# A hybrid retention/NATTEN encoder layer on one core: the output weights of mixing split once, and element-wise work moved from GpSimd to VectorE

## The chip, the cores and the metric

The kernel runs on one core of a Trainium2 chip. The metric is device time in microseconds of one execution, the median of several. The core's engines run side by side, each with its own queue of instructions in a fixed order: TensorE (PE; PEld loads its weights), VectorE (DVE), ScalarE (ACT), GpSimd (POOL), and SyncE (SP), which issues most DMAs. They wait for each other with semaphores. TensorE reads its operands from SBUF and writes PSUM banks of 128 x 512 fp32.

## The reference: what is computed

One layer of an encoder, sequence 1024, width 1024, feed-forward width 2816, all in fp32:

```python
h = _swiglu(_rms_norm(x, ffn1_pre_norm[l]), ffn1_w_in[l], ffn1_w_out[l])
x = x + 0.5 * _rms_norm(h, ffn1_post_norm[l])
m = _token_mixing(_rms_norm(x, mix_pre_norm[l]), w_mix_in[l], ..., w_mix_out[l], pos)
x = x + _rms_norm(m, mix_post_norm[l])
h = _swiglu(_rms_norm(x, ffn2_pre_norm[l]), ffn2_w_in[l], ffn2_w_out[l])
x = x + 0.5 * _rms_norm(h, ffn2_post_norm[l])
```

`_token_mixing` projects to retention and neighbourhood-attention heads, merges their gated outputs to one 1024 x 1024 matrix and multiplies it by `w_mix_out` (1024 x 1024). The change sits around this last multiplication, and where its result, after norm and residual, is prepared for the second feed-forward block.

## The kernel before

**Products.** Every fp32 matrix operand is split in two parts, high (`...h`) and low (`...l`), of a type that TensorE multiplies fast: `split` rounds to the high part on ACT (L61) and subtracts it on DVE (L62, or on POOL where `eng` says so). `mm3` then makes three multiplications, high x high (L88), high x low (L89), low x high (L90). A weight piece of 128 x 512 is loaded raw (`wraw`) by SP and split into `wh`, `wl`, which have eight buffers each; an activation piece is loaded as `graw` and split to `gh`, `gl` by `stream`.

**Strassen-Winograd.** The wide matrix products run as seven products per pair of output tiles instead of eight. For the activations this needs the four quadrants and their sums, in a `Winograd` object: a11, a12, a22, s1 = a21 + a22, s2 = s1 - a11, s3 = a11 - a21, s4 = a12 - s2, each held as high and low part. They are filled token tile by token tile (eight tiles of 128 tokens). `Ep` and its like normalise a tile; `flip` then transposes its halves with TensorE into a `pt` bank (L127) and calls `put`. Tiles 0 to 3 only give a11 and a12. Tiles 4 to 7 give the rest: with the first half, a21 is copied on ACT (L278) and S3 formed by two subtract/add operations (L282, L283); with the second half come a22 (split), s1 (L288), s2 (L290), and S4 by two operations on POOL (L293, L294) and a split whose subtract is on POOL too. The names `cmb` in the profile are the buffers of a21, s1 to s4 before their splits. `put` serves two places: the end of FFN1's output (its result feeds mixing, at about 680 to 735 us), and the end of mixing's output (its result feeds FFN2, at about 1550 to 1665 us). In the second use only, S3 of tiles 4 and 5 is on POOL (`s3_on_pool`).

**The output projection of mixing** (`out_proj`, about 1523 to 1629 us). The eight token tiles go in groups (0,1,2), (3,4,5), (6,7). For each group the eight k-blocks of the weights are loaded and split, two pieces each, and each block gives a step `one` per tile: two banks by three multiplications. The last three blocks (`tail`) are done tile by tile, so that a tile's banks end early. When a tile is done, `Ep` squares its banks on ACT (L220), forms the factor on DVE and POOL (L222, L98), multiplies (L227) and adds the residual (L229, on POOL for tiles 6 and 7), squares again (L231) and normalises (L118). The tile's transposes are then queued in `left` with a lag: they run when so many further steps have passed, eight or three after the tile before, whichever is later. A `put` that returns a function (the split of S4) is queued again for two steps later.

**The lead.** What is left of these functions after the last group is `rest`; `Pairs.lead` runs them between the first products of FFN2: four pairs of tiles, each a product with a11 and one with a12, and after each pair one function of `rest`. Then `run` goes on with each pair's s2, s3, s1, a22 and s4 products; it needs raw weights combined on DVE (L510 to L530) and evicts banks on DVE (L517, L520, ...).

**The order of the work.** The instruction order on each engine is fixed at build time by a scheduler that takes the program's order, its pools' buffers and its own estimates of durations into account. So a change at one place can reorder its neighbourhood; an instruction waiting at the head of an engine's queue holds all behind it.

**Memory.** SBUF is handed out in stacks of pools. The operands of the second `put` use lie in the pool `a2`, made before `out_proj`.

Of the kernel before, what the change touches and what calls it, by code (L numbers as in the profile page):

```python
# [18 lines left out]
P = 128  # L19
# [19 lines left out]
class Core:  # L39
# [97 lines left out]
    def out_proj(self, nk, lhs, wload, done, groups=((0, 1, 2), (3, 4, 5), (6, 7)), tail=3, lag=8, space=3):  # L137

        left = []

        def one(t, k, a, w):
            for e in [e for e in left if e[0] <= 0]:
                left.remove(e)
                f = e[1]()
                if f is not None:
                    left.append([2, f])
            for b in range(2):
                self.mm3(banks[t][b], a[t], w[b], k == 0, k == nk - 1)  # L150
            for e in left:
                e[0] -= 1

        for toks in groups:
            banks = {t: [self.bank() for _ in range(2)] for t in toks}
            tl = tail if len(toks) > 1 else 0
# [4 lines left out]
            last = [(k, lhs(k, toks), wload(k)) for k in range(nk - tl, nk)]  # L161
# [37 lines left out]
class Ep:  # L199
# [12 lines left out]
    def __call__(self, t, banks):  # L212
# [12 lines left out]
        for b in range(2):  # L225
            bs = slice(b * 512, (b + 1) * 512)
            nc.vector.scalar_tensor_tensor(y[:, bs], banks[b], r[:, 0:1], self.post[:, bs],  # L227
                                           op0=ALU.mult, op1=ALU.mult)
            (nc.gpsimd if t > 5 else nc.vector).tensor_tensor(x[:, bs], y[:, bs], x[:, bs], ALU.add)  # L229
            if self.pre is not None:  # L230
                nc.scalar.activation(y[:, bs], x[:, bs], AF.Square, scale=1.0 / 32.0, accum_out=sx[:, b:b + 1])  # L231
# [5 lines left out]
class Winograd:  # L237
# [6 lines left out]
    def __init__(self, c, pools, tmp, bufs, spill=None, order=None):  # L244

        self.c, self.tmp, self.spill, self.s3_on_pool = c, tmp, spill, ()
        self.ops = {}
        if order is not None:
            for n in order:
                self.ops[n] = [pools.tile([P, 4, 512], F32R, name=f"{n}{q}") for q in "hl"]  # L250
            return
# [8 lines left out]
    def part(self, n, ts):  # L260
        return [q[:, :, ts] for q in self.op(n)]

    def put(self, t, g, pt):
# [12 lines left out]
        if g == 0:  # L276
# [4 lines left out]
            eng = nc.gpsimd if t in self.s3_on_pool else nc.vector  # L281
            eng.tensor_tensor(self.s3, h1, self.a21, ALU.subtract)  # L282
            eng.tensor_tensor(self.s3, self.s3, l1, ALU.add)  # L283
# [9 lines left out]
        nc.gpsimd.tensor_tensor(s3, h2, s3, ALU.subtract)  # L293
        nc.gpsimd.tensor_tensor(s3, s3, l2, ALU.add)  # L294
        return lambda: c.split(*self.part("s4", ts), s3, eng=nc.gpsimd)
# [903 lines left out]
def trunk_layer(ctx: ExitStack, tc, x, xt, g1a, w1i, w1o, g1b, gma, wmt, wnv, wrv, logits, dtab, rope, bias,  # L1199
# [283 lines left out]
    a_stack = ExitStack()  # L1483
    apool = pool(a_stack, "a2", "right")
    cmb = pool(left, "cmb2")
    wx = Winograd(c, apool, cmb, None, order=("s4", "a22", "s1", "s3", "a12", "s2", "a11"))
    wx.s3_on_pool = (4, 5)
    with tc.tile_pool(name="ep2", bufs=1, reuse_waits="tile") as ep:
        rest = c.out_proj(KT, stream(c, gs, lambda k: d["m"][k]), lambda k: c.load_w(wmo[k]),
                          Ep(c, ep, gmb, g2a, False, rows(x1), rows(x2), wx.put))  # L1490
# [4 lines left out]

        fin.lead(save, rest)
# [96 lines left out]
```

## Time and profile before

| | |
|---|---|
| median of 3 runs | 2280.56 us (2280.09 to 2283.82) |
| profiled execution | 2281.11 us, its span 2279.3 us |
| mean granted TensorE clock | 0.992 |
| TensorE busy | 2209.3 us |
| DVE busy | 1662.9 us |
| ACT busy | 1000.5 us |
| POOL busy | 629.9 us |

The profile is one execution. Its time stands 1.8 us over its span. Busy times are sums over the whole run; what one stage is limited by is read from the windows and waits of that stage. A row of waits reads: engine, its line, what it waited for, us in total, times, longest. A row of groups reads: line, engine, operation, output and inputs, shape, count, busy us, mean ns, then idle time of the engine ahead of these instructions and what ended it. `<-` with an engine and a line names the instruction that released the waiting one.

### The profile page before, as it was taken

To read this page: it belongs to the slowest core of one execution; us is meant where nothing else is said; L and a number is where in the kernel's file an instruction comes from. 1 tells how busy PE (TensorE), PEld (TensorE's weight loads), DVE (VectorE), ACT (ScalarE), POOL (GpSimd) and SP (SyncE) were. 2 spreads that over 40 slices of the span, in tenths; PEclk is the share of its full clock that TensorE was granted. 3 is DMA by queue.
4 is the path that set the end of the run, shared out by engine and by line. 5 is a ranking of instruction groups with operands and counts; after the bars stand their busy time and mean duration, and the time that the engine had idled before them with its cause. 6 is when DMAs were issued, how large, how long until landed. Compare 5 with 4: busy or idle time off the path is not lost. (4 is left out here: it accounts for less than half of the span.)

```text
span 2279.3 us, 30175 instructions
## 1 busy us (share of the span) xinstructions
PE 2209.3 (97%) x10232; PEld 1830.4 (80%) x10232; DVE 1662.9 (73%) x2928; ACT 1000.5 (44%) x2086; POOL 629.9 (28%) x779
## 2 busy tenths in 40 slices
PE   7899999999998999999999999999899999999998
PEld 5678888888786887878888888887678888888886
DVE  7898878755568657769876678537988787876444
ACT  5444434332344222349875665315644343433232
POOL 1121212168424122301101222101522121115942
PEclk9999999999999999999999999999999999999999
DMA  6354434598654564557745566866535444449865
GB/s 249 134 184 145 175 130 175 197 378 293 201 178 157 176 184 128 150 174 256 218 165 165 166 217 235 292 215 208 169 134 177 161 156 158 143 146 368 304 225 181
DMA packets 152650, 448.31 MB, mean 197 GB/s; under 512 B 19312, under 2 KB 47088, under 8 KB 150384
## 3 DMA queue, kind: packets, MB, share of 16 engines
q1 hardware_dynamic: 111216, 314.23, 41.1%
q0 software_dynamic: 41280, 132.15, 16.0%
q8 instruction: 81, 1.33, 0.2%
q14 instruction: 73, 0.60, 0.1%
HBM read 305.80 MB, written 144.70 MB: 198 GB/s over the span
## 5 line engine op out<-in xcount | busy, mean ns | idle before, releaser
L62 DVE TENSOR_TENSOR wl<-wraw,wh 128x512 fp32r<-128x512 f32 x512 | 353.3, 708 | 85.4 <-ACT wh L61 84.7
L61 ACT CAST wh<-wraw 128x512 fp32r<-128x512 f32 x516 | 297.6, 618 | 192.1 <-PE ps L89 63.2
L88 PE MATMUL ps<-wh,g 128*128 128x512 f32 x484 | 188.6, 390 | 0.0
L89 PE MATMUL ps<-wl,g 128*128 128x512 f32 x484 | 188.5, 390 | 0.0
L90 PE MATMUL ps<-wh,g 128*128 128x512 f32 x484 | 188.4, 389 | 0.0
L552 ACT ACTIVATE c<-c 128x512 f32<-128x512 f32 x88 | 55.5, 632 | 204.3 <-DVE c L517 103.9
L62 DVE TENSOR_TENSOR wl<-w,wh 128x512 fp32r<-128x512 f32 x77 | 76.4, 1005 | 84.2 <-ACT wh L61 83.2
L62 DVE TENSOR_TENSOR wl<-x,wh 128x512 fp32r<-128x512 f32 x77 | 78.8, 1040 | 76.5 <-ACT wh L61 75.1
L88 PE MATMUL ps<-a11h,wh 128*128 128x512 f32 x276 | 111.6, 404 | 9.2 <-ACT wh L61 9.2
L61 ACT CAST wh<-t 128x512 fp32r<-128x512 f32 x58 | 36.0, 621 | 184.2 <-DVE t L511 184.2
L90 PE MATMUL ps<-a11h,wl 128*128 128x512 f32 x276 | 109.4, 397 | 2.6 <-DVE wl L62 2.4
L88 PE MATMUL ps<-a22h,wh 128*128 128x512 f32 x280 | 109.8, 392 | 0.0
L90 PE MATMUL ps<-a22h,wl 128*128 128x512 f32 x280 | 109.2, 390 | 0.6 <-DVE wl L62 0.6
L89 PE MATMUL ps<-a11l,wh 128*128 128x512 f32 x276 | 109.5, 397 | 0.1
L89 PE MATMUL ps<-a22l,wh 128*128 128x512 f32 x280 | 109.1, 390 | 0.0
L88 PE MATMUL ps<-a12h,wh 128*128 128x512 f32 x276 | 108.8, 394 | 0.3 <-ACT wh L61 0.3
L90 PE MATMUL ps<-a12h,wl 128*128 128x512 f32 x276 | 107.5, 390 | 0.0
L89 PE MATMUL ps<-a12l,wh 128*128 128x512 f32 x276 | 107.5, 389 | 0.0
L89 PEld LDWEIGHTS ps<-wl,g 128*128 128x128 f32 x484 | 90.9, 188 | 19.1 <-DVE wl L62 0.5
L90 PEld LDWEIGHTS ps<-wh,g 128*128 128x128 f32 x484 | 90.8, 188 | 19.0
L88 PEld LDWEIGHTS ps<-wh,g 128*128 128x128 f32 x484 | 90.9, 188 | 18.7
L88 PE MATMUL ps<-s2h,wh 128*128 128x512 f32 x232 | 91.8, 396 | 6.8 <-ACT wh L61 6.8
(433 smaller groups left out, 6443.8 us busy)
## 6 DMA issues: line engine op xcount, KB each, us to landing
wraw<-in_dram SPq DMA_DIRECT2D x218, 512.0 KB, 4.5
g<-g0s SPq DMA_DIRECT2D x44, 512.0 KB, 4.2
g<-g1s SPq DMA_DIRECT2D x44, 512.0 KB, 4.6
g<-g0a SPq DMA_DIRECT2D x33, 512.0 KB, 3.3
g<-g1a SPq DMA_DIRECT2D x33, 512.0 KB, 4.4
g0s<-gth POOLq DMA_DIRECT2D x44, 256.0 KB, 5.2
g0s<-cmb POOLq DMA_DIRECT2D x44, 256.0 KB, 3.7
g1s<-gth POOLq DMA_DIRECT2D x44, 256.0 KB, 4.9
```

The costliest lines, as they stand in the source:

```text
L61: self.done = [nc.scalar.copy(h, src).ins, (eng or nc.vector).tensor_tensor(l, src, hf, ALU.subtract).ins]
L62: (eng or nc.vector).tensor_tensor(l, src, hf, ALU.subtract).ins]
L88: mm(ps, a[0], b[0], start=start, stop=False)
L89: mm(ps, a[0], b[1], start=False, stop=False)
L90: mm(ps, a[1], b[0], start=False, stop=stop)
L552: nc.scalar.activation(gate[j], gate[j], AF.Silu)
```

## The change

The split weights of mixing's output are kept. A dictionary `held` has the eight k-blocks: blocks 0 to 3 stay in the eight `wh`/`wl` buffers, blocks 4 to 7 go to a new pool `wm` of 16 tiles. Each block is loaded and split when the first group asks for it, and only then. `wm` lies where s4 and a22 of the second `put` use lay; it is closed, and these two get their memory, when the third group asks for block 0. So that this can be, the third group takes the blocks in the order 4, 5, 6, 7, 0, 1, 2, 3.

On DVE instead of POOL run: the residual sums of tiles 6 and 7 in `Ep`, S3 of tiles 4 and 5 (`s3_on_pool` is gone), and the two operations and the low part of the split of S4, in both uses of `put`. The transposes of tile 4 wait 11 steps instead of 8 in mixing's output; those of tile 5 follow three later as before. An empty function at the head of `rest` puts the transposes of tiles 6 and 7 one pair later in the lead.

The diff, without the parts that only pass arguments (line numbers in the changed kernel: L220 becomes L218, L222 L220, L227 L225, L229 L227, L231 L229, L278 L279; the other lines named here keep theirs):

```diff
     def out_proj(...):
-            for k in range(nk - tl):
-                w, a = wload(k), lhs(k, toks)
+            for k in order[:nk - tail]:
+                w, a = wload(g, k), lhs(k, toks)
...
-                    left.append([max(lag, max([e[0] for e in left], default=-space) + space), f])
+                    left.append([max(lags.get(t, lag), max([e[0] for e in left], default=-space) + space), f])
...
-            (nc.gpsimd if t > 5 else nc.vector).tensor_tensor(x[:, bs], y[:, bs], x[:, bs], ALU.add)
+            nc.vector.tensor_tensor(x[:, bs], y[:, bs], x[:, bs], ALU.add)
...
-            eng = nc.gpsimd if t in self.s3_on_pool else nc.vector
-            eng.tensor_tensor(self.s3, h1, self.a21, ALU.subtract)
-            eng.tensor_tensor(self.s3, self.s3, l1, ALU.add)
+            nc.vector.tensor_tensor(self.s3, h1, self.a21, ALU.subtract)
+            nc.vector.tensor_tensor(self.s3, self.s3, l1, ALU.add)
...
-        nc.gpsimd.tensor_tensor(s3, h2, s3, ALU.subtract)
-        nc.gpsimd.tensor_tensor(s3, s3, l2, ALU.add)
-        return lambda: c.split(*self.part("s4", ts), s3, eng=nc.gpsimd)
+        nc.vector.tensor_tensor(s3, h2, s3, ALU.subtract)
+        nc.vector.tensor_tensor(s3, s3, l2, ALU.add)
+        return lambda: c.split(*self.part("s4", ts), s3)
...
-    wx = Winograd(c, apool, cmb, None, order=("s4", "a22", "s1", "s3", "a12", "s2", "a11"))
-    wx.s3_on_pool = (4, 5)
+    wx = Winograd(c, apool, cmb, None, order=("s1", "s3", "a12", "s2", "a11"))
+    held = {}
+
+    def wload(g, k):
+        if k not in held:
+            raw = c.raw(wmo[k])
+            held[k] = []
+            for b in range(2):
+                src = raw[:, b * 512:(b + 1) * 512]
+                if k < 4:
+                    held[k].append(c.piece(src))
+                    continue
+                held[k].append([wm.tile([P, 512], F32R, name=f"wm{q}{k}{b}") for q in "hl"])
+                c.split(*held[k][b], src)
+        if g == 2 and k == 0:
+            wm_stack.close()
+            wx.add(pool(a_stack, "a2b", "right"), ("s4", "a22"))
+        return held[k]
...
-        rest = c.out_proj(KT, stream(c, gs, lambda k: d["m"][k]), lambda k: c.load_w(wmo[k]),
-                          Ep(c, ep, gmb, g2a, False, rows(x1), rows(x2), wx.put))
+        ks = tuple(range(KT))
+        rest = c.out_proj(KT, stream(c, gs, lambda k: d["m"][k]), wload,
+                          Ep(c, ep, gmb, g2a, False, rows(x1), rows(x2), wx.put), (ks, ks, ks[4:] + ks[:4]), lags={4: 11})
...
+        rest.insert(0, lambda: None)
         fin.lead(save, rest)
```

How this moves the instructions. First DVE in the third group of mixing's output, around the normalisation of tile 5 (`tmp`, `epx`; `gl` and `wl` are the low parts of activations and weights of the group's blocks), before:

```order
L229 TENSOR_TENSOR epx_15541<-tmp_15540,epx_15541 128x512 x2
L62 TENSOR_TENSOR a22l_14809<-pt_15669,a22h_14808 128x4x128
L288 TENSOR_TENSOR cmb_15664<-pt_15669,cmb_15664 128x512
L114 TENSOR_SCALAR ss3_15549<-ss3_15549 128x1
L62 TENSOR_TENSOR wl_15695<-wraw_15692,wh_15694 128x512
L118 SCALAR_TENSOR_TENSOR tmp_15557<-epx_15541,rstd_15559,gpre_14825 128x512 x2
L62 TENSOR_TENSOR s3l_14813<-cmb_15665,s3h_14812 128x4x128
L62 TENSOR_TENSOR s1l_14811<-cmb_15664,s1h_14810 128x4x128
L290 TENSOR_TENSOR cmb_15665<-pt_15669,cmb_15665 128x512
L62 TENSOR_TENSOR wl_15699<-wraw_15692,wh_15698 128x512
L62 TENSOR_TENSOR gl_15704<-graw_15702,gh_15703 128x256
```

and now:

```order
L227 TENSOR_TENSOR epx_15460<-tmp_15459,epx_15460 128x512 x2
L62 TENSOR_TENSOR gl_15556<-graw_15554,gh_15555 128x256
L62 TENSOR_TENSOR gl_15582<-graw_15580,gh_15581 128x256
L114 TENSOR_SCALAR ss3_15468<-ss3_15468 128x1
L118 SCALAR_TENSOR_TENSOR tmp_15476<-epx_15460,rstd_15478,gpre_14824 128x512 x2
L62 TENSOR_TENSOR gl_15627<-graw_15625,gh_15626 128x256
L282 TENSOR_TENSOR cmb_15592<-a11h_14817,cmb_15591 128x512
L62 TENSOR_TENSOR a22l_15579<-pt_15596,a22h_15578 128x4x128
L283 TENSOR_TENSOR cmb_15592<-cmb_15592,a11l_14818 128x512
```

The splits `wl` of the group's weights are gone from between, the group's `gl` stand earlier, tile 4's transform starts behind tile 5's normalisation, and its S3 (L282, L283) is on DVE.

Second, DVE in the lead, around the splits of the weights of its last pair (`wl_16085`, `wl_16102` before; `wl_15930`, `wl_15947` now) and the normalisation and transform of tiles 6 and 7, before:

```order
L227 SCALAR_TENSOR_TENSOR tmp_15845<-ps_15564,rstd_15852,gpost_14823 128x512
L62 TENSOR_TENSOR wl_16047<-wraw_16043,wh_16046 128x512
L62 TENSOR_TENSOR wl_16064<-wraw_16043,wh_16063 128x512
L62 TENSOR_TENSOR wl_16085<-wraw_16081,wh_16084 128x512
L114 TENSOR_SCALAR ss3_15854<-ss3_15854 128x1
L62 TENSOR_TENSOR wl_16102<-wraw_16081,wh_16101 128x512
L118 SCALAR_TENSOR_TENSOR tmp_15862<-epx_15846,rstd_15864,gpre_14825 128x512 x2
```

and now:

```order
L62 TENSOR_TENSOR wl_15930<-wraw_15926,wh_15929 128x512
L290 TENSOR_TENSOR cmb_15842<-pt_15846,cmb_15842 128x512
L62 TENSOR_TENSOR s1l_14810<-cmb_15841,s1h_14809 128x4x128
L282 TENSOR_TENSOR cmb_15905<-a11h_14817,cmb_15904 128x512
L62 TENSOR_TENSOR s2l_14816<-cmb_15842,s2h_14815 128x4x128
L283 TENSOR_TENSOR cmb_15905<-cmb_15905,a11l_14818 128x512
L293 TENSOR_TENSOR cmb_15842<-a12h_14813,cmb_15842 128x512
L62 TENSOR_TENSOR a22l_15579<-pt_15909,a22h_15578 128x4x128
L294 TENSOR_TENSOR cmb_15842<-cmb_15842,a12l_14814 128x512
L288 TENSOR_TENSOR cmb_15904<-pt_15909,cmb_15904 128x512
L62 TENSOR_TENSOR s3l_14812<-cmb_15905,s3h_14811 128x4x128
L62 TENSOR_TENSOR wl_15947<-wraw_15926,wh_15946 128x512
```

Before, the last pair's splits stood ahead of tile 6's normalisation; now they stand behind most of the transforms of tiles 6 and 7, with S4 (L293, L294) among them.

Third, DVE at the end of FFN1's output, in the transforms of two neighbouring tiles; `wl_5999`, `wl_6016` and `wl_6071` are splits of the first held pairs of mixing's input, before:

```order
L62 TENSOR_TENSOR wl_5999<-wraw_5995,wh_5998 128x512
L62 TENSOR_TENSOR s2l_5820<-cmb_5875,s2h_5819 128x4x128
L282 TENSOR_TENSOR cmb_5946<-a11h_5217,cmb_5945 128x512
L62 TENSOR_TENSOR a22l_5806<-pt_5951,a22h_5805 128x4x128
L283 TENSOR_TENSOR cmb_5946<-cmb_5946,a11l_5218 128x512
L288 TENSOR_TENSOR cmb_5956<-pt_5951,cmb_5945 128x512
L62 TENSOR_TENSOR wl_6016<-wraw_5995,wh_6015 128x512
L62 TENSOR_TENSOR s3l_5811<-cmb_5946,s3h_5810 128x4x128
L62 TENSOR_TENSOR wl_6071<-wraw_6067,wh_6070 128x512
```

and now:

```order
L293 TENSOR_TENSOR cmb_5875<-a12h_5226,cmb_5875 128x512
L283 TENSOR_TENSOR cmb_5946<-cmb_5946,a11l_5218 128x512
L294 TENSOR_TENSOR cmb_5875<-cmb_5875,a12l_5227 128x512
L62 TENSOR_TENSOR a22l_5806<-pt_5951,a22h_5805 128x4x128
L288 TENSOR_TENSOR cmb_5956<-pt_5951,cmb_5945 128x512
L62 TENSOR_TENSOR s4l_5832<-cmb_5875,s4h_5831 128x4x128
L62 TENSOR_TENSOR s3l_5811<-cmb_5946,s3h_5810 128x4x128
L62 TENSOR_TENSOR s1l_5816<-cmb_5956,s1h_5815 128x4x128
L290 TENSOR_TENSOR cmb_5946<-pt_5951,cmb_5946 128x512
L62 TENSOR_TENSOR wl_5999<-wraw_5995,wh_5998 128x512
L62 TENSOR_TENSOR wl_6016<-wraw_5995,wh_6015 128x512
```

`wl_5999` and `wl_6016` moved behind the tile's S4 and transform, and `wl_6071` stands twelve rows further still.

One more place differs, SP's loads at the start of FFN2's output, where four loads of `g` (numbers 19513, 19554, 19590, 19608) now stand ahead of those of `w11` to `w8`; before, `w11` and `w10` stood ahead of the first of them, and `w9` ahead of the other three.

More of the change, by code (lines that the diff above doesn't have):

```diff
@@ L261, in part, with add @@
         return [q[:, :, ts] for q in self.op(n)]
+    def add(self, pool, order):
+        for n in order:
+            self.ops[n] = [pool.tile([P, 4, 512], F32R, name=f"{n}{q}") for q in "hl"]
     def put(self, t, g, pt):
```

18 lines of the change are left out of this document (9 added, 9 removed).

## The prediction

> **What bounds the kernel now.** I read the page first: the busy line, then the chain.
>
> ```profile
> span 2279.3 us, 30175 instructions
> PE 2209.3 (97%) x10232; PEld 1830.4 (80%) x10232; DVE 1662.9 (73%) x2928; ACT 1000.5 (44%) x2086; POOL 629.9 (28%) x779
> PE 35%; DVE 3%; issue 1%; POOL 1%; ACT 1%; DMA 0%; POOLq 0%; DVEq 0%; ACTq 0%
> ```
>
> TensorE is at work 97% of the span, and the change leaves its multiplications alone. So a gain can only come out of the idle 70 us (2279.3 − 2209.3) and out of time at a reduced clock. DVE at 73% is an average; the table by stage shows where it is the limit. This is the end of mixing, where the change sits (columns: window, its length, busy time of PE, PEld, DVE, ACT, POOL with counts, granted clock, DMA share, GB/s):
>
> ```profile
> 1590.00:1600.00 10.00, 9.52 (x47) 7.60 (x46) 9.38 (x18) 8.96 (x24) 2.46 (x4) 1.00 0.72 243
> 1600.00:1610.00 10.00, 6.13 (x29) 4.06 (x27) 9.10 (x16) 6.70 (x17) 5.01 (x5) 0.96 0.46 164
> 1610.00:1620.00 10.00, 7.50 (x22) 4.81 (x22) 9.68 (x14) 3.58 (x7) 6.53 (x5) 0.70 0.61 185
> 1620.00:1630.00 10.00, 7.65 (x29) 5.21 (x30) 10.00 (x13) 5.14 (x12) 5.58 (x4) 1.00 0.36 119
> 1630.00:1640.00 10.00, 8.11 (x38) 6.30 (x37) 9.42 (x16) 7.36 (x22) 5.20 (x6) 0.99 0.66 200
> 1650.00:1660.00 10.00, 10.00 (x46) 8.15 (x45) 8.25 (x14) 6.18 (x10) 5.92 (x4) 1.00 0.01 2
> ```
>
> Between 1600 and 1640 DVE is full while TensorE idles, and the clock dips to 0.70. DVE does 13 to 18 instructions in 10 us there; its own timeline says why the number varies (start, duration, instruction):
>
> ```profile
> 1602.85 2.84 DVE L229 TENSOR_TENSOR epx<-tmp,epx 128x512 f32<-128x512 f32 x2
> 1611.19 1.23 DVE L62 TENSOR_TENSOR wl<-wraw,wh 128x512 fp32r<-128x512 f32 x1
> 1623.36 4.06 DVE L62 TENSOR_TENSOR wl<-wraw,wh 128x512 fp32r<-128x512 f32 x3
> 1650.66 0.69 DVE L62 TENSOR_TENSOR s2l<-cmb,s2h 128x512 fp32r<-128x512 f32 x1
> 1651.26 0.69 DVE L283 TENSOR_TENSOR cmb<-cmb,a11l 128x512 f32<-128x512 f32 x1
> ```
>
> Undisturbed, such an instruction takes 0.69 us and the next starts 0.60 us later; the first three rows have the same shape and take 1.2 to 1.4 each. The waits of this stage (total, times, longest; 1590 to 1670, the row of tmp L227 from 1470 to 1720) name who waits for it:
>
> ```profile
> ACT s4h L61 <- POOL cmb L294: 11.9, 4, 3.9
> PE ps L89 <- DVE wl L62: 4.8, 3, 3.1
> PE pt L127 <- DVE tmp L118: 2.4, 2, 1.8
> PE ps L88 <- DVE tmp L227: 1.0, 2, 0.5
> PE ps L90 <- DVE gl L62: 1.1, 3, 0.6
> ```
>
> TensorE is held by splits and normalisations that queue on DVE; for ACT it waits a third as long.
>
> **What is removed.** The groups of instructions from 1522 to 1705 (count, then busy time and mean ns):
>
> ```profile
> L62 DVE TENSOR_TENSOR wl<-wraw,wh 128x512 fp32r<-128x512 f32 x61 | 45.2, 768 | 13.3 <-ACT wh L61 13.2
> L61 ACT CAST wh<-wraw 128x512 fp32r<-128x512 f32 x61 | 35.4, 619 | 23.6 <-PE ps L90 13.5 <-PE ps L89 4.8 <-DMA wraw<-in_dram 4.0
> L294 POOL TENSOR_TENSOR cmb<-cmb,a12l 128x512 f32<-128x512 f32 x4 | 6.9, 1723 | 0.3
> L293 POOL TENSOR_TENSOR cmb<-a12h,cmb 128x512 f32<-128x512 f32 x4 | 6.4, 1603 | 11.1 <-DVE s2l L62 11.1
> L229 POOL TENSOR_TENSOR epx<-tmp,epx 128x512 f32<-128x512 f32 x4 | 6.0, 1509 | 1.8 <-DVE tmp L227 1.8
> L62 POOL TENSOR_TENSOR s4l<-cmb,s4h 128x512 fp32r<-128x512 f32 x4 | 5.8, 1445 | 2.9 <-ACT s4h L61 2.9
> ```
>
> Three groups of tokens split eight blocks of two pieces each: 48 of these pieces; 16 stay. 32 subtracts leave DVE: 32 × 0.60 = 19.2 us of its queue, half under group 1 (from about 1555 to 1592, where TensorE hardly waits) and half under group 2. 32 casts leave ACT (32 × 0.53 us, the spacing of casts in a run such as the six in 3.21 us below, = 17 us; ACT does not bound here) and 16 loads of 512 KB leave SP and the DMA engines (8 MB at shares of 0.36 to 0.72). Casts and loads I cost at nothing: they lie beside DVE's work, and without them nothing starts later.
>
> **What is added to DVE in this stage.** Four residual adds, four S3 operations, twelve of S4: 20 × 0.60 = 12.0 us. POOL loses its four groups above, 25.1 us, and S3. Net on DVE: 19.2 − 12.0 = 7.2 us less. Beside that, DVE gets back the stretch. The three long rows alone lose 2.84 + 1.23 + 4.06 − 6 × 0.68 = 4.1 us. All stretched rows from 1602 to 1648 together come to about 9 us (estimate, by the same subtraction). The Trainium skill (GPSIMD Engine Reference, section 8, Key points) says that POOL shares its SBUF interfaces with VectorE and contends with instructions that have two SBUF inputs, which these are; the trace agrees with its 1.2 to 1.4 us against 0.69. By that rule the whole stretch goes once POOL is idle, which is what my count by rows takes too.
>
> **The sum at the end of mixing.** Two points fix the stage: the start of group 2 and the start of the s3 product of the first pair.
>
> ```profile
> 1591.93 0.39 PE L89 MATMUL ps<-wl,gh 128*128 128x512 f32 x1
> 1634.39 0.39 PE L88 MATMUL ps<-a12h,wh 128*128 128x512 f32 x1
> 1636.88 0.39 PE L90 MATMUL ps<-a12h,wl 128*128 128x512 f32 x1
> 1663.93 0.50 PE L88 MATMUL ps<-s3h,wh 128*128 128x512 f32 x1 [1.83 <-ACT wh L61]
> ```
>
> The middle two are the first and last of twelve in a row: 2.49/11 = 0.227 us a multiplication. Call 1591.9 T0; s3 starts at T0 + 72.0. TensorE's own work between is 96 multiplications of group 2 and 96 of the lead, 12 of s2 (204 × 0.227 = 46.3 us) and five tiles' transposes (about 0.92 each, 4.6): T0 + 50.9. So 21 us are lost, to waits and to the clock, and that is the most that the stage can give.
>
> Now the new queue. Group 2 begins with blocks 4 to 7, then 0 to 3, all split, so TensorE needs only the activations' low halves (gl) from DVE. I let it end at T0 + 26 (50.9 − 46.3 is transposes; 21.8 + 2.8 of them + 1.5 for a late gl and the bank of tile 7). Tile 4's transposes now come 11 steps after its end, three of them in group 1, so eight steps of 6 × 0.227 us: T0 + 10.9, and DVE starts its transform at about T0 + 12.5. From there DVE's order is a solid queue: 63 instructions up to the split of the last lead product (49 of 0.60, 8 of 0.67, 4 of about 0.13 and 2 of 0.34 = 36 us), plus four times 0.45 us for the rstd round over POOL. That split is done at T0 + 50 to T0 + 52. TensorE, unheld, would want it at T0 + 47 to 48 (26 + 16.3 for three pairs, 2.7 for half a pair, 1.8 for the two tiles). It waits 3 to 4 us. Ten rows later, at T0 + 56 to T0 + 58, DVE has the split for s2, which TensorE would reach 2 us sooner; with the last four multiplications s3 starts at about T0 + 59.5. The gain is 72.0 − 59.5 = 12.5. T0 itself comes about 1.0 us earlier, since the waits for tmp L227 are group 1's. Against that stand 1.2 us of reduced clock after the two new waits (one dip costs 1.5, by the rows at 732.38 and 736.57 below: 4.19 us for twelve multiplications instead of 2.72; I count most of one). Sum: −12.3 us; bounds −19 (no new wait, no dip) and −4 (both new waits twice as long).
>
> **The same put() at the end of FFN1's output.** S4 of four tiles moves there as well, 12 × 0.60 = 7.2 us onto a DVE that shows this:
>
> ```profile
> 700.00:710.00 10.00, 9.22 (x46) 7.36 (x44) 10.00 (x14) 6.16 (x12) 6.76 (x8) 1.00 0.48 147
> 710.00:720.00 10.00, 9.27 (x43) 7.79 (x44) 10.00 (x12) 3.92 (x7) 5.26 (x4) 1.00 0.88 305
> 714.61 1.77 DVE L282 TENSOR_TENSOR cmb<-a11h,cmb 128x512 f32<-128x512 f32 x1
> 726.25 1.62 POOL L294 TENSOR_TENSOR cmb<-cmb,a12l 128x512 f32<-128x512 f32 x1
> 732.38 0.77 PE L88 MATMUL ps<-s1h,wh 128*128 128x512 f32 x1 [3.00 <-DVE ev L520]
> 736.57 0.40 PE L88 MATMUL ps<-a22h,wh 128*128 128x512 f32 x1
> PE pt L127 <- DVE cmb L290: 1.5, 2, 1.2
> ```
>
> 26 instructions in 20 us are 0.77 each; at 0.60 they would need 15.6, so the stretch (4.4 here, about 8 in 690 to 728) pays for the moved work. The old waits of 3.0 and 1.5 go: the 3.0 was an eviction behind splits behind ACT's s4h behind POOL's 726.25. But the changed order puts the splits behind each tile's whole transform. Counting at 0.60 from the start of the second tile's transform (694.4), the split wl of the second held pair (36 rows on) ends at 716.7, where TensorE is ready at 713.4. A new wait of 3.3, with a dip of 1.5 behind it as after the old one of 3.0. Without the dip the a22 product starts at 733.9 instead of 736.6, with it at 735.4. I take −1.2; bounds −4.5 and +2.
>
> **FFN2's output.** SP's order changes at one more place: four loads of g now stand ahead of the loads of w11 to w8.
>
> ```profile
> 2046.83 0.82 SPq L689 DMA_DIRECT2D w<-in_dram  x2
> 2047.76 0.36 SPq L625 DMA_DIRECT2D g<-g1a  x1
> 2050.00:2060.00 10.00, 10.00 (x45) 8.26 (x45) 3.82 (x7) 1.96 (x4) 0.00 (x0) 1.00 1.02 420
> 2059.21 3.21 ACT L61 CAST wh<-w 128x512 fp32r<-128x512 f32 x6
> ```
>
> Before, w11 goes at 2046.83 and is wanted at 2059.21. Behind four loads that can go at 2047.8, it is issued near 2049.4 and behind 2 MB; at the 420 GB/s of the window, with w11's own 1 MB, 3 MB are in by about 2057. Zero; bounds 0 and +4 (estimate, one load's landing of 4 to 5 us).
>
> **Total.** −12.3 − 1.2 = −13.5 on the profiled execution's 2281.11, which lies 0.55 above the median of 2280.56. I forecast 2267.5, between 2267.6 from the one and 2267.1 from the other.
>
> **Rivals.** *The queue stays full* (A): the moved operations and the lead's splits keep DVE solid longer than I count, because group 2 frees DVE only for it to run into waits on transposes. Each of the two new waits at twice its size, with the clock dipping longer, gives −5: 2275.5. For it: 9.2 to 9.7 us busy in each 10 us up to 1650. Against: these readings contain the stretch.
> *All waits go* (B): DVE starts the solid part earlier than T0 + 12.5 allows, and the lead never waits: −19 and −1.2, 2261. For it: DVE has some 10 us less before T0. Against: tile 4's transposes cannot come sooner than their count of steps.
> *Slower* (C): the moved S4 at FFN1's output. The splits there are now behind 12 more instructions; if DVE's pace stays at 0.77 (the stretch being not POOL's doing but DMA's, which had a share of 0.88 in 710 to 720), 36 rows take 27.7 instead of 21.6 us, the wait of 3.3 becomes 9.4, and the same pace over the 73 rows at the end of mixing adds 12. Then 6.1 + 12 + 2 of dips − 13.5 is about 6.5 slower: 2287. It decides from a pace of about 0.72. Against it: of the windows with a full DVE, 1590 to 1600 has the most DMA (0.72), the least POOL and the most instructions (18). The rows at 1650.66 and 1651.26 do not decide it: full pace, but with DMA at 0.01.
> *The clock* (D): every wait near 3 us costs a dip. The row 1610 to 1620 gives 0.70 after the wait of 3.1, so 3 us lost there. If both new waits at mixing's end and the one at FFN1's output cost 3 us each, where I took 2.7 in all, 6.3 more are lost: 2274. The Trainium skill (TensorE: Matmul & The Clock Gate, Part 1) has the clock halve after an idle window of about 3.4 us and return after as long a busy one. Here 3.1 us of idle did it. By the rule, with the phase of the window unknown, waits of 3 to 4 us may or may not dip, which lies between my sum and D.
>
> **How the numbers follow.** Forecast (2262 to 2272) 0.45, D 0.15, A 0.15, B 0.13, C with its smaller forms 0.12. The range leaves out the far half of C and of B: 2257 to 2279. A measurement tells 0.2%, 4.6 us, from no change. Faster by that (below 2276) are the forecast, B, D and most of A: 0.82; within it 0.08 (the rest of A, the mild part of C); slower 0.10.
>
> **What would show it.** Right: no two-input DVE instruction of 512 above 0.8 us in 1590 to 1660 or 690 to 730, PE without waits in group 2, and two waits for a split wl late in the lead and at s2. Wrong: stretched DVE rows with POOL idle (C), a wait for wl above 5 us near 713, w11's cast late at 2059, or group 2 still waiting for DVE.

## The result and the profile after

The changed kernel takes 2269.09 us (median of 7 runs, 2265.56 to 2274.95); the kernel before, measured beside it on the same chip, takes 2281.91 (7 runs, 2278.42 to 2283.82). The ratio is 0.9948, with a 95% interval of 0.9939 to 0.9957: faster by about 12 us, where 13 were forecast. The profiled execution took 2266.95. Its page (busy time, share of the span, number of instructions):

```profile
span 2265.2 us, 30039 instructions
PE 2204.2 (97%) x10232; PEld 1830.1 (81%) x10232; DVE 1641.4 (72%) x2928; ACT 984.5 (43%) x2054; POOL 575.8 (25%) x747
```

TensorE executes the same 10232 instructions. DVE's number has not changed either: 32 subtracts are gone and 32 moved operations have come. Yet DVE is busy 21.5 us less: the rows take less time each. The stretched rows of 128x512 of before (10.0 us beyond 0.69 us each at the end of mixing, and about 8 at FFN1's output, as in the prediction) make most of it.

This is the end of mixing, in the same columns as the table of before:

```profile
1590.00:1600.00 10.00, 9.95 (x48) 7.97 (x47) 8.66 (x18) 4.88 (x15) 2.26 (x4) 1.00 0.48 170
1600.00:1610.00 10.00, 9.66 (x49) 7.78 (x48) 8.88 (x18) 6.11 (x14) 1.13 (x2) 1.00 0.54 188
1610.00:1620.00 10.00, 10.00 (x47) 8.23 (x47) 10.00 (x19) 8.10 (x19) 0.86 (x1) 1.00 0.07 15
1620.00:1630.00 10.00, 10.00 (x49) 8.32 (x49) 9.10 (x17) 5.10 (x14) 2.31 (x3) 1.00 0.48 168
1630.00:1640.00 10.00, 8.56 (x40) 6.31 (x39) 9.54 (x18) 5.67 (x13) 1.44 (x2) 1.00 0.20 82
1640.00:1650.00 10.00, 5.76 (x16) 3.82 (x17) 10.00 (x17) 5.21 (x9) 0.00 (x0) 0.83 0.17 52
```

From 1600 to 1630 TensorE now works almost without a break at full clock. Before, it was at 6.1 to 7.7 of 10 there, with the clock down to 0.70. DVE does 17 to 19 instructions in each window where it did 13 to 16. The remaining loss has gathered in one place, 1640 to 1650. TensorE's rows name it (start, duration, instruction, and in brackets the wait and what ended it); the first is the start of mixing's output, the second that of group 2, the third that of the lead, the last the s2 product of the fifth pair, after which nothing differs:

```profile
1521.00 0.39 PE L88 MATMUL ps<-wh,gh 128*128 128x512 f32 x1
...
1590.69 0.39 PE L89 MATMUL ps<-wml,gh 128*128 128x512 f32 x1
...
1616.64 0.39 PE L88 MATMUL ps<-a11h,wh 128*128 128x512 f32 x1
...
1636.37 0.50 PE L90 MATMUL ps<-a11h,wl 128*128 128x512 f32 x1 [1.05 <-DVE wl L62]
...
1642.98 0.50 PE L90 MATMUL ps<-a12h,wl 128*128 128x512 f32 x1 [3.38 <-DVE wl L62]
1647.84 0.50 PE L88 MATMUL ps<-s2h,wh 128*128 128x512 f32 x1 [0.85 <-ACT wh L61]
1648.99 0.50 PE L90 MATMUL ps<-s2h,wl 128*128 128x512 f32 x1 [0.41 <-DVE wl L62]
1651.39 0.39 PE L88 MATMUL ps<-s3h,wh 128*128 128x512 f32 x1
...
1706.35 0.39 PE L88 MATMUL ps<-s2h,wh 128*128 128x512 f32 x1
```

The same two ends in the profile of before:

```profile
1522.70 0.39 PE L88 MATMUL ps<-wh,gh 128*128 128x512 f32 x1
...
1720.47 0.39 PE L88 MATMUL ps<-s2h,wh 128*128 128x512 f32 x1
```

I call the time between these ends "the stage": 197.8 us before, 185.4 after. This is −12.4. Two groups of DVE in it (mean ns last before the idle time) show that the stretch is gone; the splits had a mean of 768 ns before:

```profile
L62 DVE TENSOR_TENSOR wl<-wraw,wh 128x512 fp32r<-128x512 f32 x27 | 18.0, 687 | 0.2 <-ACT wh L61 0.2
L227 DVE TENSOR_TENSOR epx<-tmp,epx 128x512 f32<-128x512 f32 x16 | 10.4, 684 | 0.0
```

Where the rest of the span's 14.1 us went: +0.1 up to the a22 product at FFN1's output (below), −1.8 from there to the start of mixing's output, where both kernels do the same. That second stretch took 783.2 to 788.5 us in the thirteen profiles told of here, with no order by kernel (786.1 and 786.7 in two of before), so it is the spread of executions and not the change. From the fifth pair's s2 product to the end all thirteen take 558.8 or 558.9 us.

At FFN1's output the windows and the two rows that decide are these:

```profile
700.00:710.00 10.00, 9.32 (x44) 6.70 (x43) 9.86 (x17) 6.30 (x13) 3.63 (x6) 1.00 0.76 241
710.00:720.00 10.00, 6.65 (x28) 5.11 (x27) 9.76 (x18) 3.33 (x6) 0.00 (x0) 0.94 0.43 142
720.00:730.00 10.00, 10.00 (x41) 8.17 (x40) 7.85 (x14) 3.41 (x6) 0.56 (x1) 0.89 0.47 161
```

```profile
717.67 0.50 PE L90 MATMUL ps<-a11h,wl 128*128 128x512 f32 x1 [3.35 <-DVE wl L62]
...
736.65 0.39 PE L88 MATMUL ps<-a22h,wh 128*128 128x512 f32 x1
```

DVE does 35 instructions in 20 us where it did 26, at its full pace beside a DMA share of 0.76. But TensorE waits 3.35 us for the split of the second held pair, and the clock dips behind it (0.6 + 1.1 = 1.7 us lost, from 0.94 and 0.89 of 10 us each). The a22 product starts where it started before (736.57).

And at FFN2's output, SP's loads and ACT's first split of w11:

```profile
2030.22 1.81 SPq L625 DMA_DIRECT2D g<-g1a  x4
2032.72 3.54 SPq L689 DMA_DIRECT2D w<-in_dram  x4
```

```profile
2045.09 3.73 ACT L61 CAST wh<-w 128x512 fp32r<-128x512 f32 x7
```

The four loads of g go first, w11 follows 2.5 us later. The cast stands 14.1 us earlier than before (2059.21), just as the whole span: nothing is lost.

### The profile page after: what moved, and what is told of

Its sections match the earlier page's. It is cut to its first block, busy times and chain, and to the rows that moved or that the text cites. A ratio compares the mean times of both kernels' runs of the same rounds, so it can differ in the third digit from the quotient of the medians.

```text
span 2265.2 us, 30039 instructions
## 1 busy us (share of the span) xinstructions
PE 2204.2 (97%) x10232; PEld 1830.1 (81%) x10232; DVE 1641.4 (72%) x2928; ACT 984.5 (43%) x2054; POOL 575.8 (25%) x747
## 5 line engine op out<-in xcount | busy, mean ns | idle before, releaser
L62 DVE TENSOR_TENSOR wl<-wraw,wh 128x512 fp32r<-128x512 f32 x472 | 317.1, 689 | 66.3 <-ACT wh L61 66.0
L61 ACT CAST wh<-wraw 128x512 fp32r<-128x512 f32 x476 | 274.2, 618 | 169.2 <-PE ps L89 69.2
```

The lines of the kernel that those rows point to most:

```text
L61: self.done = [nc.scalar.copy(h, src).ins, (eng or nc.vector).tensor_tensor(l, src, hf, ALU.subtract).ins]
L62: (eng or nc.vector).tensor_tensor(l, src, hf, ALU.subtract).ins]
```

## The experiments

The theory: DVE's queue holds TensorE at the end of mixing, and the gain comes from two halves, 32 subtracts less and no stretch, since POOL no longer runs two-input work beside it. The rivals: one half alone makes the gain; or the new order of the transposes does. For FFN1's output, the theory is that the late splits ate what the moved S4 gave. In the table, the stage is that of each run's profile (mixing: from the first multiplication of its output to the fifth pair's s2; FFN1: from the first tile's transposes to the a22 product), and the ratio is to the kernel before, with its interval.

| kernel | median us | ratio | mixing | FFN1 |
|---|---|---|---|---|
| before | 2281.91 | 1 | 197.8 | 57.8 |
| after | 2269.09 | 0.9948 (0.9939 to 0.9957) | 185.4 | 58.1 |
| held_only | 2279.00 | 0.9989 (0.9980 to 0.9998) | 197.4 | 57.3 |
| held_insert_old | 2276.71 | 0.9970 (0.9959 to 0.9982) | 196.2 | 54.9 |
| moves_only | 2277.26 | 0.9979 (0.9969 to 0.9990) | 196.7 | 57.5 |
| s4_pool_mix | 2274.95 | 0.9972 (0.9961 to 0.9984) | 193.9 | 60.7 |
| res_pool | 2270.08 | 0.9950 (0.9937 to 0.9962) | 188.3 | 57.1 |
| insert_old | 2270.56 | 0.9947 (0.9935 to 0.9959) | 190.0 | 57.3 |
| s4_pool_ffn1 | 2268.67 | 0.9942 (0.9930 to 0.9954) | 187.1 | 57.2 |
| both_early | 2264.66 | 0.9922 (0.9909 to 0.9935) | 189.9 | 51.2 |
| s4_late | 2265.06 | 0.9918 (0.9905 to 0.9932) | 186.6 | 52.1 |
| leads_early | 2262.36 | 0.9910 (0.9895 to 0.9925) | 187.4 | 51.3 |
| before_again | 2280.23 (one) | – | 199.2 | 57.3 |

The stage of one order spreads: 185.4, 187.1 and 187.4 in three kernels whose mixing is written alike, 197.8 and 199.2 in two profiles of before. So differences below 2 us in that column say nothing. At FFN1's output one order spreads over 3 us: 57.1 to 60.7 for that of the changed kernel, 54.9 to 57.8 for that of before. The profile of s4_pool_mix, with the 60.7, is of its slowest run (2280.70). The medians were not all measured on one chip; the ratios compare them.

**held_only: the weights kept, the moved work back on POOL.** Residual sums, S3 of tiles 4 and 5 and S4 go back to POOL, the rest of the change stays.

```diff
-            nc.vector.tensor_tensor(x[:, bs], y[:, bs], x[:, bs], ALU.add)
+            (nc.gpsimd if t > 5 else nc.vector).tensor_tensor(x[:, bs], y[:, bs], x[:, bs], ALU.add)
...
-            nc.vector.tensor_tensor(self.s3, h1, self.a21, ALU.subtract)
-            nc.vector.tensor_tensor(self.s3, self.s3, l1, ALU.add)
+            eng = nc.gpsimd if self.spill is None and hasattr(self, "late") and t < 6 else nc.vector
+            eng.tensor_tensor(self.s3, h1, self.a21, ALU.subtract)
+            eng.tensor_tensor(self.s3, self.s3, l1, ALU.add)
...
-        nc.vector.tensor_tensor(s3, h2, s3, ALU.subtract)
-        nc.vector.tensor_tensor(s3, s3, l2, ALU.add)
-        return lambda: c.split(*self.part("s4", ts), s3)
+        eng = nc.gpsimd if True else nc.vector
+        eng.tensor_tensor(s3, h2, s3, ALU.subtract)
+        eng.tensor_tensor(s3, s3, l2, ALU.add)
+        return lambda: c.split(*self.part("s4", ts), s3, eng=eng)
...
+    wx.late = True
```

> The changed kernel, with the residual sums of tiles 6 and 7, S3 of tiles 4 and 5 and S4 back on POOL; the weights stay split once and the transposes stay late. Theory (DVE's queue is the bound at mixing's end; its length counts, and both the splits and the stretch beside POOL lengthen it): the 9.6 us of splits under the third group are gone, the stretch is not; 5 to 9 us of the 12.8 gained, about 2274, with DVE rows of 1.2 us and more back around 1600 to 1660. Rival 1 (contention with POOL was nearly all): at most 4 us gained, 2278 or more. Rival 2 (the weights are all of it): 11 us or more, 2271 or less.

0.9989: 2.5 us, the figure of the first rival; the 5 to 9 of the theory were missed. The waits from 1590 to 1670 (line numbers one or two higher than in the changed kernel):

```profile
PE pt L127 <- DVE cmb L291: 7.2, 2, 6.4
PE pt L127 <- DVE tmp L118: 3.5, 1, 3.5
ACT s4h L61 <- POOL cmb L296: 8.9, 4, 2.9
```

TensorE hardly waits for splits any more (0.3 us), but for the transforms and the normalisation of tile 6. POOL's and DVE's timelines say why these are late:

```profile
1618.81 1.67 POOL L227 TENSOR_TENSOR epx<-tmp,epx 128x512 f32<-128x512 f32 x1 [0.86 <-DVE tmp L225]
1620.45 1.74 POOL L295 TENSOR_TENSOR cmb<-a12h,cmb 128x512 f32<-128x512 f32 x1
1622.27 1.62 POOL L296 TENSOR_TENSOR cmb<-cmb,a12l 128x512 f32<-128x512 f32 x1
1623.84 1.74 POOL L227 TENSOR_TENSOR epx<-tmp,epx 128x512 f32<-128x512 f32 x1
```

```profile
1619.91 6.22 DVE L62 TENSOR_TENSOR wl<-wraw,wh 128x512 fp32r<-128x512 f32 x4
...
1629.03 1.41 DVE L118 SCALAR_TENSOR_TENSOR tmp<-epx,rstd,gpre 128x512 f32<-128x512 f32 x2 [0.47 <-POOL rstd L98]
```

The second half of tile 6's residual sum stands in POOL's queue behind an S4, and during these four POOL rows four splits on DVE take 6.22 us instead of 2.5 (four starts 0.60 apart and 0.68 for the last). Tile 6 is normalised 14.3 us after the lead began; in the changed kernel it is 8.9. All of DVE's stretched rows of this stage come to 10.9 us, about as much as before (10.0).

**moves_only: the moved work on DVE, the weights split for each group as before.**

```diff
-            (nc.gpsimd if t > 5 else nc.vector).tensor_tensor(x[:, bs], y[:, bs], x[:, bs], ALU.add)
+            nc.vector.tensor_tensor(x[:, bs], y[:, bs], x[:, bs], ALU.add)
...
-        nc.gpsimd.tensor_tensor(s3, h2, s3, ALU.subtract)
-        nc.gpsimd.tensor_tensor(s3, s3, l2, ALU.add)
-        return lambda: c.split(*self.part("s4", ts), s3, eng=nc.gpsimd)
+        nc.vector.tensor_tensor(s3, h2, s3, ALU.subtract)
+        nc.vector.tensor_tensor(s3, s3, l2, ALU.add)
+        return lambda: c.split(*self.part("s4", ts), s3)
...
-    wx.s3_on_pool = (4, 5)
```

> The kernel before, with only the element-wise work moved from POOL to DVE; weights split three times, transposes as before. Theory: 12.0 us more on a full DVE at mixing's end against some 9 us of stretch that goes: 0 to 5 us slower than before, about 2285, with all DVE rows at 0.69. Rival 1 (contention was the loss): 5 us or more faster than before, 2277 or less. A third outcome, 10 us or more slower, would say that the stretch is not POOL's doing.

0.9979, 4.8 us faster, which is nearly the rival's 5 or more; the theory had it slower or the same. The profile has no stretched DVE row left, but waits in group 2 of much the same size as before, the longest 2.8 us where it was 3.1 (windows, then waits of 1590 to 1670):

```profile
1600.00:1610.00 10.00, 5.95 (x24) 3.90 (x22) 9.54 (x18) 6.11 (x13) 1.44 (x2) 0.83 0.46 166
1610.00:1620.00 10.00, 8.05 (x28) 5.92 (x27) 9.22 (x18) 4.82 (x10) 0.00 (x0) 0.83 0.49 146
```

```profile
PE pt L127 <- DVE tmp L118: 5.0, 3, 2.8
PE ps L90 <- DVE wl L62: 2.4, 1, 2.4
PE ps L88 <- ACT wh L61: 1.9, 1, 1.9
```

DVE at full pace, 18 instructions in each window, still is full, and TensorE idles beside it. In the stage the profile gives 196.7 against 198.5 (the mean of the two of before): of the 4.8 us only 1.8 are seen there, the rest of that profile's gain lies in the stretch that both kernels share. Together with the run before this one: the two halves alone give 1.1 and 1.8 us of the stage (198.5 − 197.4 and − 196.7), and both at once 11.9 (198.5 less 186.6, the mean of three). By the ratios it is 2.5 and 4.8 against 11.9. Neither half is the cause by itself: the intervals of both lie above that of the change. With the splits alone taken out, tile 6 comes late through POOL's queue; with the work alone taken off POOL, TensorE waits for normalisations and splits in a full DVE queue. Whether the two halves add up is less clear. The stage columns say no (1.1 and 1.8 against 11.9). But they are single profiles, and held_insert_old, further down, has the weights kept with the transposes at their old place: its ratio gives 6.8 us, which with the 4.8 here makes 11.6, against 12.1 for insert_old, which has both.

**s4_pool_mix and res_pool: which of the moves counts.** The first puts S4 back on POOL in mixing alone, the second the residual sums of tiles 6 and 7.

```diff
-        nc.vector.tensor_tensor(s3, h2, s3, ALU.subtract)
-        nc.vector.tensor_tensor(s3, s3, l2, ALU.add)
-        return lambda: c.split(*self.part("s4", ts), s3)
+        eng = nc.gpsimd if self.spill is None else nc.vector
+        eng.tensor_tensor(s3, h2, s3, ALU.subtract)
+        eng.tensor_tensor(s3, s3, l2, ALU.add)
+        return lambda: c.split(*self.part("s4", ts), s3, eng=eng)
```

> The changed kernel with S4 back on POOL at mixing's end only (residual sums, S3 on DVE; weights kept). Theory (in held_only the normalisation of tiles 6 and 7 came late because the residual sums queue behind S4 on POOL and DVE's splits stretch beside it; with the residual on DVE only the stretch is left): 3 to 6 us slower than the changed kernel, 2272 to 2275. Rival 1 (S4 on POOL alone undoes the gain): 8 us or more slower. Rival 2 (the residual sums alone matter): within 2 us.

```diff
-            nc.vector.tensor_tensor(x[:, bs], y[:, bs], x[:, bs], ALU.add)
+            (nc.gpsimd if t > 5 else nc.vector).tensor_tensor(x[:, bs], y[:, bs], x[:, bs], ALU.add)
```

> The changed kernel with only the residual sums of tiles 6 and 7 back on POOL (S3, S4 on DVE; weights kept). Theory (an idle POOL starts them at once; two take 3.0 us instead of 1.3 for each tile, and DVE's instructions beside them stretch by some 2 us): 1 to 4 us slower than the changed kernel. Rival (the residual sums are what holds the lead): 6 us or more slower.

S4 is worth 5.5 us (0.9972 less 0.9948, of 2282; the intervals do not touch), as expected. Its waits and two of the stretched DVE rows:

```profile
PE pt L127 <- DVE cmb L290: 4.1, 1, 4.1
PE ps L88 <- ACT s2h L61: 3.2, 1, 3.2
ACT s4h L61 <- POOL cmb L295: 7.3, 4, 2.1
```

```profile
1627.24 1.10 DVE L62 TENSOR_TENSOR wl<-wraw,wh 128x512 fp32r<-128x512 f32 x1
1628.27 1.77 DVE L227 TENSOR_TENSOR epx<-tmp,epx 128x512 f32<-128x512 f32 x1
```

At 1626.14, 1627.87 and 1630.22 POOL starts an operation of S4 of 1.6 us each, and the DVE rows beside them take 1.1 to 1.8 us; in all 5.6 us of stretch. The residual sums alone cost 1 us or nothing: the intervals overlap, and 188.3 is less than 2 us above the others. Yet in this profile too four rows on DVE, at 1619.23, 1620.27, 1627.84 and 1629.24, take 1.1 to 1.8 us beside them, 3.4 us of stretch in all. So stretch need not cost time; it does where TensorE waits for what stands behind it. S3 of tiles 4 and 5 was not put back alone.

**insert_old and held_insert_old: the transposes of tiles 6 and 7 at their old pair,** in the changed kernel and in held_only.

```diff
-        rest.insert(0, lambda: None)
```

> The changed kernel without the empty function at the head of the lead's list, so the transposes of tiles 6 and 7 run one pair earlier. Theory (tile 6 is normalised about 9 us after the lead's start in the changed kernel, and its transposes stand after the second pair, 10.9 us of multiplications; after the first pair, at 5.4, they would wait some 3 to 4 us, and the last pair's split still be late): 1 to 4 us slower. Rival (it makes no difference, TensorE loses the same wait elsewhere): within 1 us.

> The kernel of held_only (weights kept, element-wise work on POOL) without the empty function at the head of the lead's list, so that the transposes of tiles 6 and 7 run one pair earlier again. Theory (held_only's trace: TensorE waits 6.4 us with tile 7's transposes for L290 of tile 6, which stands behind buffers that S4 on POOL frees late; late transposes and S4 on POOL together make that wait): 3 to 6 us faster than held_only, 2273 to 2276. Rival (DVE rows stretched beside POOL bound the lead, wherever the transposes stand): within 2 us of held_only's 2279.

In the changed kernel the ratio is the same (0.9947), the rival's figure and not the theory's 1 to 4 us, though the profile has one long wait instead of two shorter ones:

```profile
1645.51 0.79 PE L90 MATMUL ps<-a11h,wl 128*128 128x512 f32 x1 [6.90 <-DVE wl L62]
```

By the runs it cannot be told from no change. In held_only the early place is better by 2 to 4 us (medians and ratios), with intervals that just touch, so the later place may have cost something there; the profiles do not show it. The stage is 1.2 us shorter, inside its spread, and another 2.4 us stand at FFN1's output, where both kernels have the same instructions in the same order. The reason that I gave, buffers that S4 frees late, is not what the profile shows either:

```profile
1629.61 1.94 PE L127 MATMUL pt<-ident,tmp 128*128 128x128 f32 x8 [9.52 <-DVE tmp L118]
```

TensorE stands before tile 6's transposes for its normalisation, which is late through POOL's queue.

**before_again.** The kernel before, profiled a second time.

> The kernel before, unchanged, for a second profile. The stretch from 1003 to 1521 us, where nothing was changed, took 519.2 us in the first profile of before and 516.3 to 517.5 in five others. If that was that one execution, this profile shows about 517 too; if it belongs to the kernel before, about 519.

The stage took 199.2 and the unchanged stretch 786.7. The first windows again show TensorE idle beside a full DVE:

```profile
1600.00:1610.00 10.00, 4.76 (x20) 2.94 (x18) 9.54 (x14) 5.74 (x12) 6.20 (x6) 0.86 0.45 163
```

So the losses there belong to the kernel. The unchanged stretch by itself would put the 1.8 us down to the kernel too. But s4_pool_ffn1 and s4_late, with the changed order, took 788.5 there, and moves_only, with the old one, 783.2. It is the spread of executions.

**s4_pool_ffn1, both_early, leads_early: FFN1's output.** The first puts S4 back on POOL there alone (`self.spill is not None` in the edit of s4_pool_mix). The second gives the splits of the lead, in mixing and at FFN1's output, a priority 60 rows earlier; the third does it at FFN1's output alone:

```diff
     def products(...):                                      # both_early alone
-        bs = [b if isinstance(b, tuple) else self.c.piece(b, eng) for b in bs]
+        with self.c.tc.high_priority(offset=60) if self.saved == 1 and self.last is None else nullcontext(): bs = [b if isinstance(b, tuple) else self.c.piece(b, eng) for b in bs]
...
     def leads(...):                                         # both
-                b = self.c.piece(g[:, j * 512:(j + 1) * 512])
+                with self.c.tc.high_priority(offset=60): b = self.c.piece(g[:, j * 512:(j + 1) * 512])
```

> The changed kernel with S4 back on POOL at the end of FFN1's output only. Theory (the trace: the stage took 0.3 us longer than before, the wait for the late split wl taking the place of the old waits): the same as the changed kernel within 1 us, the wait for wl near 713 gone and the one for the eviction L520 near 729 back. Rival (the moved S4 costs what the new wait costs, 3.5 us and a dip): 3 to 5 us faster than the changed kernel.

> The changed kernel with the splits of the lead's weights given a higher priority in both stages, so that DVE does them before the transforms. Theory (the two late splits are the waits that are left: 3.5 and 1.2 us with dips of 1.2 at mixing's end, 3.5 with 1.6 at FFN1's): 5 to 9 us faster than the changed kernel, about 2262. Rival (DVE is full either way, the wait only moves to the s2 and s3 products): within 2 us of the changed kernel.

> The changed kernel with the early splits only at the end of FFN1's output (mixing's end as in the changed kernel). Theory (both_early's trace: that stage was 6.9 us shorter, while mixing's end got 4.6 us longer, because the wait moved to the s2 product): 6 to 8 us faster than the changed kernel, about 2262. Rival (both_early's gain came half from mixing): 2 to 4 us faster, about 2266.

With S4 on POOL at FFN1's output the time is the same (0.9942 against 0.9948). The wait for wl near 713 is gone, and the old one of 3.00 for the eviction is back. So the moved S4 there gained nothing because its price came back as the late split. With the splits early as well (leads_early), the stage is 6.8 us shorter and the kernel 6.7 us faster by the medians (2262.36 against 2269.09), 8.7 by the ratios; 6 to 8 were expected. Early splits with S4 on POOL there were not run, so how much of this needs the move is open. The window of leads_early:

```profile
710.00:720.00 10.00, 9.90 (x44) 7.91 (x43) 10.00 (x18) 3.19 (x6) 0.56 (x1) 1.00 0.50 189
```

TensorE is at 9.90 where it was at 6.65, at full clock, with not one wait between 700 and 735. DVE was busy 9.76 there and is 10.00: its work is the same, in another order. both_early is 4.4 us faster than the changed kernel by the medians, just under the 5 to 9 expected, and its gain stands at FFN1's output alone (51.2). At the end of mixing the same treatment seems to do harm (189.9 against 185.4 to 187.4; the intervals of both_early and leads_early overlap): one wait in place of two, longer than each,

```profile
1642.82 0.79 PE L88 MATMUL ps<-s2h,wh 128*128 128x512 f32 x1 [5.55 <-ACT wh L61]
```

with the clock at 0.67 from 1640 to 1650. There DVE's queue is full up to the s2 product (9.76 of 10 us busy), and a split done sooner makes another late. leads_early beats both kernels: 0.9910, 20 us faster than before.

**s4_late: leads_early, and S4 of tiles 6 and 7 behind the first combined weight of the lead.**

```diff
-        nc.vector.tensor_tensor(s3, h2, s3, ALU.subtract)
-        nc.vector.tensor_tensor(s3, s3, l2, ALU.add)
+        def last():
+            with c.tc.high_priority(offset=-40):
+                nc.vector.tensor_tensor(s3, h2, s3, ALU.subtract)
+                nc.vector.tensor_tensor(s3, s3, l2, ALU.add)
+                c.split(*self.part("s4", ts), s3)
+        if self.late and t > 5: return last
...
```

> leads_early, and S4 of tiles 6 and 7 at mixing's end put behind the first combined weight of FFN2 (t2) on DVE instead of among the transforms: same work, other order. Theory (DVE's order in front of the last lead split and of the s2 product is what is left; six of its instructions are needed only at the s4 product): the split comes 1.2 us and t2's split 2.4 us sooner, s3 starts 3 to 4 us sooner; 2258 to 2260. Rival (the wait only moves on, to the evictions or to s4): within 1 us of leads_early.

2265.06, not 2258 to 2260. The s2 product starts 2.0 us sooner after the lead's start, and 2.4 us come back later, among them a wait where the moved work now stands:

```profile
1655.03 0.50 PE L90 MATMUL ps<-a22h,wl 128*128 128x512 f32 x1 [1.07 <-DVE wl L62]
```

By its mechanism the rival was right, that the wait only moves on; its figure, within 1 us, was not quite (2.7 us slower than leads_early by the medians, 1.8 by the ratios, whose intervals overlap). Not tried: tile 4's transposes at their old 8 steps, since s4 and a22 of mixing get their memory only when group 2 asks for block 0.

## Why the prediction was right

**The end of mixing, −12.3, measured −12.4.** With T0 = 1590.69 in the changed kernel: the lead starts at T0 + 25.95 (forecast 26), the last late split is there at T0 + 52.3 (50 to 52), s2 starts at T0 + 57.2 (56 to 58), s3 at T0 + 60.7. The step from 72.0 to 60.7 is −11.3, what 59.5 and the 1.2 of dips came to. The two waits are 3.38 and 1.26 (0.85 and 0.41 at s2), where 3 to 4 and 2 were forecast, with one of 1.05 ahead of them that I had not counted. The dip takes 1.7 us from the window 1640 to 1650, not 1.2.

**T0 1.0 us earlier: wrong.** From the start of mixing's output to T0 it took 69.2 us before and takes 69.7. Only one wait for tmp L227, 0.5 us, was group 1's, and three short ones (0.5, 0.4, 0.2) took its place. That 1.5 us came back behind s3, which I had not counted at all: 1.1 from s3 to the second pair (the wait of 0.66 for wl there is gone) and 0.5 in the pairs up to the fifth. So the total is as close as it is by two errors that cancel, and the last tenth is luck anyway: the same order took 1.7 and 2.0 us longer in two other profiles.

**The stretch goes with POOL's work: right.** No two-input row of DVE in the stage is above 0.8 us, against 10.0 us of excess before (9 in the estimate). The prediction's 1.2 to 1.4 us a row are means of merged rows; singly, the rows inside take 0.7 us or 1.1 to 1.8. Rival C, that DMA makes the stretch, falls with 0.60 a row at a DMA share of 0.76, and held_only and s4_pool_mix bring it back beside POOL's rows. The Trainium skill (GPSIMD Engine Reference, section 8, Key points) has this contention as a rule, and here the trace agrees both ways.

**The sum took the two halves as additive, and the runs leave that open.** 7.2 us less of work and 9 less of stretch shorten DVE's queue, and I let every microsecond of it count. In the stage of single profiles either half alone brings 1 to 2 us, far from additive; by the ratios the halves bring 2.5 or 6.8 us (held_only, held_insert_old) and 4.8 (moves_only), which nearly adds up with the 6.8. Shown is only that neither half alone gives the 12.

**FFN1's output, −1.2, measured +0.1 at the a22 product, inside the bounds.** The wait is 3.35 (forecast 3.3) and the dip 1.7 (1.5); what was off is when that wait begins and ends, each 0.9 us late. The split ended at 717.6 instead of 716.7 because DVE's queue waited for ACT in small pieces (0.32 us for s1h at 699.53, 0.24 for s2h at 710.32, two of 0.15), and TensorE was ready at 714.3 instead of 713.4, after other waits of 0.3 to 0.7 us. In the profile's total the missing 1.2 us are hidden by the 1.8 of the unchanged stretch.

**FFN2's output, 0: right.** The load of w11 follows at once behind the four of g.

**The clock** (rival D) cost 1.7 + 1.7 = 3.4 us where 2.7 were counted. A (the waits doubled) and B (none) did not come.

## What to carry to other kernels

When an engine's queue holds TensorE, count what is left of the queue after the edit, not what is taken out: with either relief alone the kernel gained 2.5 to 6.8 us, with both 12, and in the profiles of the halves TensorE stands in the same stage for the next late row. Two-input work put on POOL to help DVE can cost DVE about as much time as it saves (10.0 us of stretch here, against 12.0 us of rows), so look for long rows of a known shape before sharing work so. And after a move, look at what now stands behind the moved rows: here the order of the held splits was worth 6.7 us, half as much as the change itself.

## What the hardware showed beside this

The contention does not always fall on DVE. A 128x512 fp32 operation with two inputs in SBUF takes 0.69 us on DVE in the changed kernel and in moves_only, and 1.27 to 1.31 on POOL where nothing is in its way. Side by side the rows look in two ways. Here DVE gives way (s4_pool_mix):

```profile
1620.29 1.29 POOL L295 TENSOR_TENSOR cmb<-cmb,a12l 128x512 f32<-128x512 f32 x1
1620.34 1.79 DVE L62 TENSOR_TENSOR s3l<-cmb,s3h 128x512 fp32r<-128x512 f32 x1
```

and here POOL does (before):

```profile
1653.18 2.32 POOL L294 TENSOR_TENSOR cmb<-cmb,a12l 128x512 f32<-128x512 f32 x1
1653.66 0.69 DVE L62 TENSOR_TENSOR wl<-t,wh 128x512 fp32r<-128x512 f32 x1
```

In the two stages (690 to 735, 1590 to 1672) of all thirteen profiles, 131 such DVE rows start inside such a POOL row. 120 of them end 0.54 to 0.56 us after the POOL row ends, whenever they started, so they wait for it. In the other 11 the POOL row itself lasts 2.3 to 2.7 us and DVE keeps 0.68 or 0.69. A DVE row with an input in PSUM (`pt`, `ps`) keeps 0.67 to 0.69 beside POOL, 68 times out of 68. Which of the two gives way can turn on very little: at FFN1's output held_only and held_insert_old have the same order, but POOL's row at 720.83 is held for 2.67 us in the one and takes 1.46 at 722.26 in the other, and TensorE's wait for the eviction behind it is 3.05 or 1.04. With the dip behind the longer wait, this is where the 2.4 us between their stages come from.

A wait of 3.35 to 3.38 us was followed by a dip of 1.7 us in two places, as one of 3.0 had been before. The Trainium skill (TensorE: Matmul & The Clock Gate, Part 1) puts the idle window at about 3.4 us; the waits here are a little shorter and dip all the same. From 650 to 760 and from 1500 to 1730 in all thirteen profiles, every wait of 2.3 us or more was followed by a dip, and so were some much shorter: before has one behind a wait of 1.79 us at 1639.06, and none behind 1.83 at 1663.93. Pieces of idle time just ahead of the waits may count, which no run here shows. Nor does the wait set the dip's length: after 3.31 us at FFN1's output, in the order of the changed kernel, s4_pool_mix shows half clock for 6.83 us where the changed kernel, after 3.35, shows it for 3.41. With a second dip of twice the length, at 691.29, this makes its stage there 60.7 us instead of 58.1.
